# Neighbourhood attention by blocks of grid columns: half the latent keys per query tile

## The chip, the cores and the metric

The kernel runs on one core of one Trainium2 chip. The metric is the device time of one execution in microseconds (us); lower is better. The engines are TensorE (PE, its weight loads PEld), VectorE (DVE), ScalarE (ACT), GpSimd (POOL) and SyncE (SP, which issues most DMAs).

## The reference

Two layers of a hybrid transformer over 512 latent tokens (a grid of 8 rows by 64 columns, numbered row by row) and 256 context tokens, width 1024. Each layer normalises the tokens, projects them once, splits the projection among four attention branches, gates and merges the branches, projects back, and then runs a mixture of 32 experts. The branches have four query heads of 64:

- A: latent attention with a low-rank key and value, dense over all keys;
- B: banded: a latent query sees latent keys at a distance of at most 128, and a sink logit;
- C: two-dimensional neighbourhood: with 8 rows the window takes in every row, and 16 columns;
- D: dense, with normalised and rotated queries and keys.

A latent query reads its latent keys and all 256 context keys in one softmax; context queries read only context keys (in layer 0 alone). For branch C, cut to what matters:

```python
c_start = jnp.clip(q_col - NA_KW // 2, 0, GRID_W - NA_KW)          # NA_KW = 16, GRID_W = 64
col_ok = (k_col[None] >= c_start[:, None]) & (k_col[None] < c_start[:, None] + NA_KW)
bias = rpb[:, dr, dc]                  # learned, by row and column distance
s = q @ [keys, context keys] * scale + [bias, 0];  s = where(mask, s, -1e30);  p = softmax(s);  o = p @ values
```

A query in column c so reads keys of columns within some 8 of c, 16 columns of 64, in all 8 rows.

## The kernel before

Weights and activations are kept as two parts, H (rounded to TensorE's fp32r) and L (the remainder), and a product is the sum of three (`mm3`, L305: H.H, H.L, L.H). The normalised tokens lie transposed in `hlat` (latent tokens, 512 columns in token order) and `hctx` (context tokens); `hsl` (L557) takes a slice of them.

A layer has a dense part (`dense`, L501: norms, projections, attention, gates, merge), an output projection (`out_proj`, L1178) and the experts (`moe`). In the dense part TensorE runs its instructions in the order in which the program writes them (`manual_schedule`, L471); the other engines' orders are the compiler's. A planner (`Flow`, L142) sets that written order: work is cut into items (`Item`, L136) with dependencies, a latency to keep after them, a need for PSUM banks and a number of SBUF slots. It keeps a model clock `clk`, to which each product adds its modelled time (`mat`, L243), and models when banks come free from tuned latencies (`LT`, L1878). When no item can go on, it puts in a piece of the filler: the gate projections with, in layer 0, the modulation products (`gates`, L1061, `mod_seg`, L397). The filler also runs ahead of ready items up to a share (`FILL`, 0.8 in layer 0 and 0.4 in layer 1) of the main work done. So the order of all attention work hangs on the modelled lengths.

Branch C (`branch_c`, L717) runs in two halves of two heads. Per half `qk` (L721) projects queries and keys transposed (`projT`, L575: weights stationary, 512 latent columns of `hlat` moving; result 128 channels by 512 tokens in one bank) and writes them with one ScalarE and one VectorE pass per head and part. The values of both halves come from `val` (L741): per token tile of 128 the tokens are stationary and 256 weight columns move, and two ScalarE copies write `V`. `bias_c` (L994) loads per head a table of 896 columns by a POOL-queue DMA and folds the column mask in on VectorE.

`attend` (L959) makes for each group g of 256 queries (g = 0, 1 latent, g = 2 context) two query tiles of 128 times two heads. Per tile `scores` (L1002):

- multiplies the query tile with the keys, latent and context columns apart, two products each (high and low key part; three in branch A), into one of two buffers `sps`. Branch C sees 512 latent columns, branch B 384 (`kts`, L967), the ends of the band masked;
- takes the minimum (scores are negated): for B and C over the context part (L1023), then a pass that adds the bias or the band mask and takes the minimum over the latent part (L1030);
- takes the exponent with the sum (L1040), the reciprocal (L1044) and the division (L1045) into `P`;
- transposes `P` by 128 columns on TensorE, three to a bank (L1056), and evicts each bank to `PT` on ScalarE (L1057).

`values` (L979) then multiplies `PT` with `V`, one key tile after the other from 0 on, both heads side by side in the array, 256 queries to a product, in plain float; one VectorE copy (L989) takes the sum out of the bank to the buffer `oT` (one of the eight of tag `t1`) and SP stores it in DRAM (L990). The merge (`merge`, L1093) reads these tensors back in the order B, A, C, D (L1111) after the attention. The trace counts two entries for each plain-float product.

## Time and profile before

| | |
|---|---|
| median of 3 runs | 2233.65 us (2231.22 to 2238.22) |
| the profiled execution | 2233.26 us |
| its span, first to last instruction | 2231.2 us |
| mean granted TensorE clock | 0.969 |
| busy: PE / PEld | 2071.0 us (93%) / 1529.6 us (69%) |
| busy: DVE / ACT / POOL | 1292.9 us (58%) / 798.7 us (36%) / 306.4 us (14%) |
| moved by DMA | 431.44 MB |

Busy time is the time in which an engine has at least one instruction under way; the shares are of the span. The clock is given as a share of full speed, 2.4 GHz. All that follows is worked out on the profiled execution.

### The profile page before, as it was taken

What the parts mean: (1) busy time and instruction counts of PE and PEld (TensorE: products, weight loads), DVE (VectorE), ACT (ScalarE), POOL (GpSimd) and SP (SyncE); (2) the same over time, 40 slices, a digit from 0 to 9 for tenths busy, and PEclk for the clock granted to TensorE, in tenths of its full rate; (3) what the DMA queues carried; (4) which work ended last, traced back from release to release, by engine and by line L of the source; (5) the groups of instructions that cost most, each with busy time, mean ns of one, the idle gap of its engine ahead of it and who ended that gap; (6) DMA issues with size and microseconds to landing.
All of it is one profiled execution on the core that took longest, in us unless ns stands there. A gap on an engine that the chain in (4) does not pass through costs nothing. (4 is left out here: it accounts for less than half of the span.)

```text
span 2231.2 us, 34132 instructions
## 1 busy us (share of the span) xinstructions
PE 2071.0 (93%) x13033; PEld 1529.6 (69%) x13033; DVE 1292.9 (58%) x2641; ACT 798.7 (36%) x1805; POOL 306.4 (14%) x325
## 2 busy tenths in 40 slices
PE   5899999999999997969999979999999998799997
PEld 2777877787888877934444468877888787644443
DVE  2545354436555565677777766555466466746655
ACT  2345355435445221212222235465455432212112
POOL 1301100001100144230000031000020013200000
PEclk8899999999999999979999989999999999899999
DMA  8234343433414655679999423112212377699992
GB/s 288 93 135 171 112 163 133 159 133 135 137 60 121 201 192 198 228 255 405 364 365 364 176 78 106 54 48 90 90 46 86 121 259 250 239 369 408 407 408 88
DMA packets 141925, 431.44 MB, mean 193 GB/s; under 512 B 19328, under 2 KB 32016, under 8 KB 141760
## 3 DMA queue, kind: packets, MB, share of 16 engines
q1 hardware_dynamic: 127264, 388.89, 48.1%
q0 software_dynamic: 13056, 35.10, 4.8%
q10 hardware_dynamic: 1440, 5.24, 0.6%
q8 instruction: 104, 1.70, 0.3%
q14 instruction: 61, 0.50, 0.1%
HBM read 399.19 MB, written 36.78 MB: 195 GB/s over the span
## 5 line engine op out<-in xcount | busy, mean ns | idle before, releaser
L250 PE MATMUL bk<-hT,wH 128*128 128x512 f32 (+1 forms) x1760 | 481.5, 361 | 5.8 <-ACT wH L274 4.6
L250 PEld LDWEIGHTS bk<-hT,wH 128*128 128x128 f32 x1760 | 299.7, 190 | 53.3 <-issue 9.0
L250 PE MATMUL bk<-hT,wL 128*128 128x512 f32 (+1 forms) x880 | 312.1, 355 | 2.8 <-DVE wL L275 2.8
L250 PE MATMUL bk<-wH,hT 128*128 128x256 f32 x1312 | 257.0, 290 | 3.8 <-DVE hT L550 1.9
L1674 DVE TENSOR_TENSOR x<-x,sps 128x1024 f32<-128x1024 f32 x166 | 195.4, 1216 | 100.4 <-PE sps L1673 99.8
L1615 PE MATMUL bk<-e,xT 128*64 128x512 f32 x1056 | 244.8, 601 | 0.0
L250 PEld LDWEIGHTS bk<-wH,hT 128*128 128x128 f32 x1312 | 213.2, 195 | 9.3 <-DVE sk L275 2.1
L275 DVE TENSOR_TENSOR wL<-wraw,wH 128x1024 fp32r<-128x1024 f32 x112 | 141.7, 1272 | 108.5 <-PE bk L250 56.1
L250 PE MATMUL bk<-wL,hT 128*128 128x256 f32 x656 | 187.9, 286 | 0.0
L250 PEld LDWEIGHTS bk<-hT,wL 128*128 128x128 f32 x880 | 166.4, 189 | 29.2 <-DVE wL L275 5.6
L274 ACT ACTIVATE wH<-wraw 128x1024 fp32r<-128x1024 f32 x132 | 138.5, 1058 | 133.3 <-DMA wraw<-in_w_gate_dram 40.3
L1615 PEld LDWEIGHTS bk<-e,xT 128*64 128x64 f32 x1056 | 72.0, 138 | 142.0 <-issue 127.5
L1040 ACT ACTIVATE P<-sps,m 128x768 f32<-128x768 f32 (+2 forms) x160 | 126.4, 791 | 75.0 <-DVE m L1020 50.8
L1673 PE MATMUL sps<-yeH,to 128*128 128x512 f32 x332 | 142.0, 428 | 2.8 <-ACT yeH L274 1.4
L1057 ACT ACTIVATE pt<-bk 128x384 f32<-128x384 f32 (+1 forms) x288 | 121.0, 466 | 65.5 <-PE bk L255 64.7
L321 POOL TENSOR_TENSOR rr<-rs,mhalf 128x1 f32<-128x1 f32 (+1 forms) x72 | 53.9, 750 | 611.1 <-DVE rs L317 537.8
L1673 PE MATMUL sps<-yeL,to 128*128 128x512 f32 x332 | 131.2, 395 | 1.7 <-DVE yeL L275 1.7
L255 PE MATMUL bk<-ident,P 128*128 128x128 f32 x800 | 119.1, 277 | 12.3 <-ACT pt L1057 5.5
L250 PEld LDWEIGHTS bk<-wL,hT 128*128 128x128 f32 x656 | 128.2, 195 | 0.5
L1638 PE MATMUL bk<-e,gT 128*64 128x512 f32 x528 | 122.3, 606 | 1.5 <-ACT gT L1631 1.5
L255 PEld LDWEIGHTS bk<-ident,P 128*128 128x128 f32 x800 | 90.8, 140 | 39.5 <-ACT pt L1057 10.8
L1621 ACT ACTIVATE eth<-bk 128x256 f32<-128x256 f32 x33 | 12.7, 384 | 284.5 <-PE bk L1615 284.5
(331 smaller groups left out, 3637.0 us busy)
## 6 DMA issues: line engine op xcount, KB each, us to landing
e<-in_w_dram SPq DMA_DIRECT2D x384, 512.0 KB
wmod<-in_w_mod_dram SPq DMA_DIRECT2D x96, 512.0 KB
wraw<-in_w_gate_dram SPq DMA_DIRECT2D x64, 512.0 KB
wraw<-in_w_in_dram SPq DMA_DIRECT2D x36, 512.0 KB
thd<-th SPq DMA_DIRECT2D x64, 256.0 KB
thm<-thd SPq DMA_DIRECT2D x32, 384.0 KB
wraw<-in_w_br_dram SPq DMA_DIRECT2D x16, 512.0 KB
wraw<-in_w_out_dram SPq DMA_DIRECT2D x16, 512.0 KB
```

Source lines behind the costliest of these rows:

```text
L250: return self.nc.tensor.matmul(out, lhsT, rhs, **kw)
L255: return self.nc.tensor.transpose(out, src, self.ident if ident is None else ident)
L274: nc.scalar.activation(H, src, AF.Copy)
L275: (eng or nc.vector).tensor_tensor(L, src, H.bitcast(F32), op=ALU.subtract)
L321: self.nc.gpsimd.tensor_tensor(r[:, :n], o[:, :n], self.mhalf.to_broadcast([128, n]), op=ALU.pow)
L1040: nc.scalar.activation(Pt[:, :n], S[:, lo:768], AF.Exp, scale=-1.0, bias=m, accum_out=sm)
L1057: nc.scalar.activation(PT[gi][:, :w, qi * 128:(qi + 1) * 128], v, AF.Copy)
L1615: nc.tensor.matmul(box["h"][64 * z:64 * z + 64, :], xT(k, z), W(z, k // 2)[:, (k % 2) * 512:(k % 2 + 1) * 512], start=k == 0, stop=k == 7, ...
L1621: nc.scalar.activation(th[s], H[s, :256], AF.Tanh, scale=0.5)
L1638: nc.tensor.matmul(Y[n][64 * z:64 * z + 64, :], gT[:, k, 64 * z:64 * z + 64], W(z, 4 + k)[:, n * 512:(n + 1) * 512], start=k == 0, stop=k ...
L1673: nc.tensor.matmul(ps[:, c], to[s, t * 128:(t + 1) * 128], w[s, c], start=i == 0, stop=i == 1)
L1674: nc.vector.tensor_tensor(self.x1[t] if out is None else out, self.x1[t], ps, op=ALU.add)
```

## The change

The latent tokens of branch C are taken in the order (block of 8 grid columns, row, column in block) instead of row by row. Queries are kept rotated by one block, so that query tile u holds the blocks 2u+1 and 2u+2 (the last one 7 and 0), and sees two key tiles of 128: u and u+1, the last one 0 and 3. The order arises in the projection, which reads `hlat` by columns (`by_column`); the values are projected transposed like the keys and turned back on TensorE (`valT`). One bias table per head serves the three inner tiles and one the wrapped tile; both heads' tables are one load of 1024 columns with the mask in it, negated on ScalarE. In branch B the first and the last query tile see two key tiles instead of three. `values` starts with key tile 4 and ends with 5, and gives a key tile's product only those queries that see it. The neighbourhood output is put back into row order by four copies and by the store. The constant `cmask` goes. Cut to its core:

```diff
+    blk = lambda cbs: (np.repeat(np.arange(8)[None], 8, 0).T[None].repeat(len(cbs), 0).reshape(-1),
+                       (8 * np.array(cbs)[:, None, None] + np.arange(8)[None, None]).repeat(8, 1).reshape(-1))
+    tabs = []
+    for qb, kb in (((1, 2), (0, 1, 2, 3)), ((7, 0), (0, 1, 6, 7))):
+        (qr, qc), (kr, kc) = blk(qb), blk(kb)
+        c0 = np.clip(qc - 8, 0, 48)[:, None]
+        ok = (kc[None] >= c0) & (kc[None] < c0 + 16)
+        dc = np.clip(kc[None] - qc[:, None], -15, 15) + 15
+        tabs.append(np.where(ok, rpb_c[:, :, kr[None] - qr[:, None] + 7, dc], np.float32(-BIG)))
+    r["rpb"] = f(np.stack(tabs, 3).reshape(NL, 2, 2, 128, 512).transpose(0, 1, 3, 2, 4).reshape(NL, 2, 128, 1024))
...
+    def by_column(self, hl, k, t0, n):
+        if t0 >= 512:
+            return self.hsl(hl, k, t0, n)
+        return self.hlat[hl][k // 2][:, k % 2].rearrange("p (r b c) -> p b r c", r=8, b=8)
...
         ps = self.bank()
         c = slice(c0, c0 + 128)
-        self.mm3(ps[:, :n], [(W(0, k)[:, c], W(1, k)[:, c], self.hsl(0, k, t0, n), self.hsl(1, k, t0, n))
-                             for k in range(8)])
+        out = ps[:, :n]
+        if t0 == 0:
+            out = out.rearrange("p (b r c) -> p b r c", r=8, c=8)
+        self.mm3(out, [(W(0, k)[:, c], W(1, k)[:, c], self.by_column(0, k, t0, n), self.by_column(1, k, t0, n))
+                       for k in range(8)])
         return ps
...
                 if part == 0:
                     q = hf.q(t0, n)
-                    nc.scalar.activation(q[own, j], ps[own, :n], AF.Copy, scale=-0.125)
-                    nc.vector.scalar_tensor_tensor(q[oth, j], ps[own, :n], -0.125, q.bitcast(F32)[own, j],
-                                                   op0=ALU.mult, op1=ALU.subtract)
+                    for d, s, m in ((0, 64, 448), (448, 0, 64)) if t0 == 0 else ((0, 0, n),):
+                        d, s = slice(d, d + m), slice(s, s + m)
+                        nc.scalar.activation(q[own, j, d], ps[own, s], AF.Copy, scale=-0.125)
+                        nc.vector.scalar_tensor_tensor(q[oth, j, d], ps[own, s], -0.125, q.bitcast(F32)[own, j, d],
+                                                       op0=ALU.mult, op1=ALU.subtract)
...
+        def valT(i):
+            ps = self.projT(box["u", 5], 128 * i, 0, 512)
+            f.use("bk", self.LT["cacc"])
+            vT = [self.t1("vT") for _ in range(2)]
+            for z in range(2):
+                nc.scalar.activation(vT[z], ps[:, 256 * z:256 * z + 256], AF.Copy)
+            yield self.LT["kt"], ("bk",)
+            v = self.transposed([vT[t // 2][:, t % 2 * 128:t % 2 * 128 + 128] for t in range(4)])
+            f.use("bk", self.LT["vacc"])
+            nc.scalar.activation(box[i].V[:, 0:4], v, AF.Copy)
         vals = []
         for hb in range(2):
             load, new = self.load_unit(box, 4 + 2 * hb), self.new_half(box, hb, "m")
-            bias = f.item(self.nop(0, lambda hb=hb: box.__setitem__(("bt", hb), [self.bias_c(2 * hb + j)
-                                                                                for j in range(2)])), slots=2)
+            bias = f.item(self.nop(0, lambda hb=hb: box.__setitem__(("bt", hb), self.bias_c(hb))), slots=1)
             pre = [load, new, bias]
             ps = []
             for t0, n in ((0, 512), (512, 256)):
...
                 new1 = self.new_half(box, 1, "m", "v")
                 new1.slots = 0
                 lv = self.load_unit(box, 5)
-                vals = [f.item(val(t), deps=[lv, new, new1], lat=self.LT["load"], need=("bk",)) for t in range(6)]
+                vals = [f.item(v, deps=[lv, new, new1] + self.norms, lat=self.LT["load"], need=("bk",))
+                        for v in [valT(i) for i in range(2)] + [val(t) for t in (4, 5)]]
                 pre += [new1, lv]
                 proj += vals + [f.item(self.nop(4), deps=vals)]
-            out.append((pre, proj, lambda hb=hb, ps=ps: self.attend("c", 2, hb, box, ps + vals, None), 7))
+            out.append((pre, proj, lambda hb=hb, ps=ps: self.attend("c", 2, hb, box, ps + vals, None), 6))
         return out
...
+    def keys(self, br, u):
+        if br == "b":
+            return list(range(max(u - 1, 0), min(u + 2, 4)))
+        if br == "c":
+            return [u, u + 1] if u < 3 else [0, 3]
+        return list(range(4))
     def attend(self, br, n, hb, box, qs, ks):
         f = self.fl
         items = []
         for g in range(3 if self.wc else 2):
-            kts = [4, 5]
-            if g < 2:
-                kts = list(range(g, g + 3) if br == "b" else range(4)) + kts
-            groups = [kts[i:i + 3] for i in range(0, len(kts), 3)]
+            see = [self.keys(br, 2 * g + qi) + [4, 5] if g < 2 else [4, 5] for qi in range(2)]
+            kts = [t for t in see[0] if t < 4] + [t for t in see[1] if t < 4 and t not in see[0]] + [4, 5]
+            groups = [kts[:-2], [4, 5]] if len(kts) == 5 else [kts[i:i + 3] for i in range(0, len(kts), 3)]
             PT = [[], []]
             tiles = []
             for qi in range(2):
-                deps = qs if ks is None else [qs[2 * g + qi]] + [ks[t] for t in kts]
+                deps = qs if ks is None else [qs[2 * g + qi]] + [ks[t] for t in see[qi]]
                 for j in range(2):
-                    tiles.append(f.item(self.scores(br, hb, box, j, g, qi, groups, PT[j]), deps=deps, lat=self.LT["evac"],
-                                        need=("S", "P")))
-            items += tiles + [f.item(self.values(n, hb, box, g, kts, PT), deps=tiles, lat=self.LT["pv"], need=("bk",))]
+                    tiles.append(f.item(self.scores(br, hb, box, j, g, qi, see[qi], groups, PT[j]), deps=deps,
+                                        lat=self.LT["evac"], need=("S", "P")))
+            items += tiles + [f.item(self.values(br, n, hb, box, g, see, groups, PT), deps=tiles, lat=self.LT["pv"],
+                                     need=("bk",))]
         return items
-    def values(self, n, hb, box, g, kts, PT):
-        f, hf = self.fl, box[hb]
+    def values(self, br, n, hb, box, g, see, groups, PT):
+        f, hf, nc = self.fl, box[hb], self.nc
         acc = self.bank()
         f.use("bk", self.LT["oacc"])
-        for i, kt in enumerate(kts):
+        at = [(gi, i, kt) for gi, grp in enumerate(groups) for i, kt in enumerate(grp)]
+        at = at[-2:-1] + at[:-2] + at[-1:]
+        for gi, i, kt in at:
+            q = [qi for qi in range(2) if kt in see[qi]]
+            c = slice(128 * q[0], 128 * q[-1] + 128)
             for j in range(2):
-                self.mat(acc[64 * j:64 * j + 64, :256], hf.v(j, kt), PT[j][i // 3][:, i % 3, :],
-                         start=i == 0, stop=i == len(kts) - 1, tile_position=(0, 64 * j))
+                self.mat(acc[64 * j:64 * j + 64, c], hf.v(j, kt), PT[j][gi][:, i, c],
+                         start=kt == 4, stop=kt == 5, tile_position=(0, 64 * j))
         f.left["pt1"] += len(PT[0]) + len(PT[1])
         oT = self.t1("oT")
-        self.nc.vector.tensor_copy(oT, acc[:, :256])
-        self.nc.sync.dma_start(self.ob[n][hb][:, g * 256:(g + 1) * 256], oT)
+        out = self.ob[n][hb]
+        if br == "c" and g < 2:
+            rows = oT.rearrange("p (r b c) -> p r b c", r=8, b=4)
+            src = acc[:, :256].rearrange("p (b r c) -> p b r c", b=4, r=8)
+            for b in range(4):
+                nc.vector.tensor_copy(rows[:, :, b], src[:, b])
+            grid = out[:, :512].rearrange("p (r c) -> p r c", r=8)
+            for b, m, c0 in ((0, 4, 8),) if g == 0 else ((0, 3, 40), (3, 1, 0)):
+                nc.sync.dma_start(grid[:, :, c0:c0 + 8 * m], oT.rearrange("p (r x) -> p r x", r=8)[:, :, 8 * b:8 * b + 8 * m])
+            return
+        nc.vector.tensor_copy(oT, acc[:, :256])
+        nc.sync.dma_start(out[:, g * 256:(g + 1) * 256], oT)
         return
         yield
-    def bias_c(self, h):
...
-    def scores(self, br, hb, box, j, g, qi, groups, PT):
+    def bias_c(self, hb):
+        bt = self.slot(name="bt")
+        self.nc.gpsimd.dma_start(bt, self.a["rpb"][self.l, hb])
+        self.nc.scalar.activation(bt, bt, AF.Copy, scale=-1.0)
+        return bt.rearrange("p (j w k) -> p j w k", j=2, w=2)
+    def scores(self, br, hb, box, j, g, qi, see, groups, PT):
         nc, f, hf = self.nc, self.fl, box[hb]
         lat = g < 2
-        k0, kn = (g * 128, 384) if br == "b" else (0, 512)
-        lo = 512 - kn if lat else 512
-        q0 = g * 256 + qi * 128
+        u = 2 * g + qi
+        kts = see[:-2]
+        kn = 128 * len(kts)
+        lo = 512 - kn
         S = self.sps()
         f.use("S", self.LT["S"] + (self.LT["Sb"] if br in "bc" and lat else 0.0))
         f.left["P"] -= 1
-        q = hf.q(q0, 128)[:, j]
-        for c0, cn, kk in ([(lo, kn, k0)] if lat else []) + [(512, 256, 512)]:
-            self.mat(S[:, c0:c0 + cn], q, hf.kh(0, j, kk, cn), start=True, stop=False)
-            self.mat(S[:, c0:c0 + cn], q, hf.kh(1, j, kk, cn), start=False, stop=br != "a")
+        wrap = br == "c" and u == 3
+        q = hf.q(u * 128, 128)[:, j]
+        for c0, cn, k0 in ([(lo, kn, 128 * kts[0])] if lat else []) + [(512, 256, 512)]:
+            out = S[:, c0:c0 + cn]
+            if wrap and k0 == 0:
+                out = out.rearrange("p (t n) -> p t n", t=2)
+                kk = lambda z: hf.kh(z, j, 0, 512).rearrange("p (t n) -> p t n", t=4)[:, 0:4:3]
+            else:
+                kk = lambda z: hf.kh(z, j, k0, cn)
+            self.mat(out, q, kk(0), start=True, stop=False)
+            self.mat(out, q, kk(1), start=False, stop=br != "a")
             if br == "a":
-                self.mat(S[:, c0:c0 + cn], hf.qr(q0, 128)[:, j], self.KR[:, kk:kk + cn], start=False, stop=True)
+                self.mat(out, hf.qr(u * 128, 128)[:, j], self.KR[:, k0:k0 + cn], start=False, stop=True)
         m = self.tiny.tile([128, 1], F32, name="m", tag="m", bufs=4)
         if br in "ad" or not lat:
             nc.vector.tensor_reduce(m, S[:, lo:768], axis=AX.X, op=ALU.min)
...
             m0 = self.tiny.tile([128, 1], F32, name="m0", tag="m0", bufs=4)
             nc.vector.tensor_reduce(m0, S[:, 512:768], axis=AX.X, op=ALU.min)
             if br == "b":
-                o = {0: 2, 1: 1, 2: 1, 3: 0}[2 * g + qi]
-                bias = self.bmask[:, o * 128:o * 128 + 384]
+                o = 128 * (kts[0] - u) + 256
+                bias = self.bmask[:, o:o + kn]
             else:
-                u = 7 - 2 * (2 * g + qi) - 1
-                bias = box["bt", hb][j][:, u:u + 8].rearrange("p u c -> p (u c)")
+                bias = box["bt", hb][:, j, int(wrap)]
             nc.vector.tensor_tensor_reduce(out=S[:, lo:512], in0=S[:, lo:512], in1=bias, op0=ALU.add,
                                            op1=ALU.min, scale=1.0, scalar=m0, accum_out=m)
         if br == "b":
...
             elif qi == 0:
                 PT += [self.sm.tile([128, 3, 256], F32, name="pt", tag="pt", bufs=NPT) for _ in groups]
                 f.left["pt1"] -= len(groups)
-            w = len(grp)
+            own = [i for i, kt in enumerate(grp) if kt in see]
+            i0, w = own[0], len(own)
             f.use("bk", self.LT["pt"])
-            v = self.transposed([Pt[:, (gi * 3 + i) * 128:(gi * 3 + i + 1) * 128] for i in range(w)])
-            nc.scalar.activation(PT[gi][:, :w, qi * 128:(qi + 1) * 128], v, AF.Copy)
+            v = self.transposed([Pt[:, see.index(grp[i]) * 128:see.index(grp[i]) * 128 + 128] for i in own])
+            nc.scalar.activation(PT[gi][:, i0:i0 + w, qi * 128:(qi + 1) * 128], v, AF.Copy)
         f.left["P"] += 1
```

## Rows read from the trace of the kernel before

**Rows 1.** Busy time by engine in stretches of the span (windows).

```profile
core 0: us, PE busy (x) PEld busy (x) DVE busy (x) ACT busy (x) POOL busy (x), PEclk, DMA share, GB/s
...
100.00:800.00 700.00, 688.58 (x4893) 568.63 (x4892) 351.89 (x826) 313.60 (x760) 70.40 (x101) 1.00 0.42 144
...
1300.00:1875.00 575.00, 545.57 (x3362) 461.02 (x3362) 336.83 (x745) 278.32 (x645) 62.06 (x64) 0.99 0.31 103
```

**Rows 2.** Instructions on tile `th`: count, duration ns min/median/max, first and last start.

```profile
L1087 ACT ACTIVATE th<-bk,hb x96: 454/687/725, 95.6 to 1852.7; 128x512 f32<-128x512 f32 x64, 128x256 f32<-128x256 f32 x32
```

**Rows 3.** PE's waits, 1325 to 1850 us: total us, times, longest us.

```profile
PE bk L255 <- ACT pt L1057: 4.7, 9, 1.1
```

**Rows 4.** Timeline of PE, layer 0's branch C: start us, us, instructions merged.

```profile
490.96 1.15 PE L255 MATMUL bk<-ident,P 128*128 128x128 f32 x9
491.86 0.71 PE L250 MATMUL bk<-hT,wH 128*128 128x512 f32 x2
...
492.64 0.39 PE L250 MATMUL sps<-kh,sq 128*128 128x512 f32 x1
492.87 0.39 PE L250 MATMUL sps<-kl,sq 128*128 128x512 f32 x1
493.09 0.28 PE L250 MATMUL sps<-sc,sq 128*128 128x256 f32 x1
...
493.33 0.63 PE L250 MATMUL bk<-hT,wH 128*128 128x512 f32 x2
...
494.11 2.81 PE L250 MATMUL bk<-pt,V 128*64 128x256 f32 x24
496.86 0.73 PE L250 MATMUL bk<-hT,wH 128*128 128x512 f32 x2
```

**Rows 5.** Timeline of PE, layer 0's branch B.

```profile
133.20 0.51 PE L250 MATMUL sps<-sk,sq 128*128 128x384 f32 x2
133.55 0.40 PE L250 MATMUL sps<-sc,sq 128*128 128x256 f32 x2
133.79 0.40 PE L250 MATMUL bk<-hT,wH 128*128 128x256 f32 x2
```

**Rows 6.** Timeline of all engines around one call of `values`.

```profile
423.79 3.33 PE L250 MATMUL bk<-pt,V 128*64 128x256 f32 x24
...
425.07 0.49 ACT L1057 ACTIVATE pt<-bk 128x384 f32<-128x384 f32 x1
```

**Rows 7.** Groups by line and form: count, busy us, mean ns, idle before and releasers.

```profile
L255 PE MATMUL bk<-ident,P 128*128 128x128 f32 x800 | 119.1, 277 | 12.3 <-ACT pt L1057 5.5 <-DVE rs L317 2.0 <-ACT V L683 1.6
...
L1057 ACT ACTIVATE pt<-bk 128x384 f32<-128x384 f32 x224 | 100.7, 490 | 55.0 <-PE bk L255 54.6
...
L250 PE MATMUL bk<-pt,V 128*64 128x256 f32 x800 | 96.2, 384 | 0.0
...
L250 PEld LDWEIGHTS bk<-pt,V 128*64 128x64 f32 x800 | 54.2, 136 | 34.3 <-issue 4.0 <-ACT pt L1057 1.6 <-ACT sq L616 0.7
...
L1030 DVE CUSTOM_DVE_ANT_0 sps<-sps,bt,m 128x512 f32<-128x512 f32 x32 | 24.3, 758 | 1.0
...
L1057 ACT ACTIVATE pt<-bk 128x256 f32<-128x256 f32 x64 | 23.5, 382 | 10.4 <-PE bk L255 10.1
...
L1030 DVE CUSTOM_DVE_ANT_0 sps<-sps,bmask,m 128x384 f32<-128x384 f32 x32 | 20.0, 624 | 0.6
...
L989 DVE COPY oT<-bk 128x256 f32<-128x256 f32 x40 | 16.9, 422 | 38.9 <-PE bk L250 38.6
```

**Rows 8.** Groups by line and form, DVE alone (L603 reads runs of 8, L601 of 32).

```profile
L603 DVE TENSOR_TENSOR r<-bk,rope_a 128x32 f32<-128x32 f32 x32 | 4.6, 181 | 0.1
...
L601 DVE TENSOR_TENSOR r<-bk,rope_a 128x32 f32<-128x32 f32 x8 | 1.4, 180 | 0.0
```

**Rows 9.** DMA issues: count, KB each, median us from issue to landing.

```profile
bt<-in_rpb_dram POOLq DMA_DIRECT2D x8, 448.0 KB, 3.5
...
rcol<-modd POOLq DMA_DIRECT2D x6, 4.0 KB, 6.8
```

More of the change, by code (lines that the diff above doesn't have):

```diff
@@ L59, in consts @@
     cs = np.clip(qc - 8, 0, 48)
-    c["cmask"] = np.where((kc >= cs) & (kc < cs + 16), 0.0, BIG).astype(np.float32)
     c["tri"] = (a < b).astype(np.float32)
@@ L113, in prep @@
     r["sink"] = f(sink_b)
-    pad = np.zeros((NL, 4, 15, 128), np.float32)
-    pad[..., 48:79] = rpb_c
-    qc, kc = np.arange(64)[:, None], np.arange(64)[None, :]
-    sk = pad[..., kc - qc + 63]
-    bt = np.stack([sk[:, :, 1:15], sk[:, :, 0:14]], 2)
-    r["rpb"] = f(bt.transpose(0, 1, 2, 4, 3, 5).reshape(NL, 4, 128, 14 * 64))
+    blk = lambda cbs: (np.repeat(np.arange(8)[None], 8, 0).T[None].repeat(len(cbs), 0).reshape(-1),
[8 more added lines that the diff above has]
+    r["rpb"] = f(np.stack(tabs, 3).reshape(NL, 2, 2, 128, 512).transpose(0, 1, 3, 2, 4).reshape(NL, 2, 128, 1024))
     r["g_qd"], r["g_kd"] = f(g_q_d), f(g_k_d)
@@ L359, in rest @@
             self.bmask = ld("bmask", [128, 640])
-            self.cmask = ld("cmask", [128, 64])
             self.iota = ld("iota", [128, 64])
@@ L991, in values @@
+        nc.vector.tensor_copy(oT, acc[:, :256])
+        nc.sync.dma_start(out[:, g * 256:(g + 1) * 256], oT)
         return
         yield
-    def bias_c(self, h):
-        nc = self.nc
-        bt = self.slot(name="bt")[:, :896].rearrange("p (u c) -> p u c", u=14)
-        nc.gpsimd.dma_start(bt.rearrange("p u c -> p (u c)"), self.a["rpb"][self.l, h])
-        nc.vector.scalar_tensor_tensor(bt, bt, -1.0, self.cmask[:, None, :].to_broadcast([128, 14, 64]),
-                                       op0=ALU.mult, op1=ALU.add)
-        return bt
```

## The prediction, made before the changed kernel was run

> **What bounds the kernel now.** I read the stretches first [rows 1]. From 100 to 800 us (layer 0's projections, attention and most of its merge) TensorE is busy 688.58 of 700 us, from 1300 to 1875 us (the same work of layer 1) 545.57 of 575, at a granted clock of 1.00 and 0.99, so at the 2.4 GHz level. VectorE has 351.89 and 336.83 us in these stretches, ScalarE 313.60 and 278.32, the DMA engines a share of 0.42 and 0.31: TensorE alone is full. The reason is in the code: the planner fills every gap of the attention with the gate projections. Next I looked for the point at which this filling runs out. The activations that end the gates' products run from 95.6 to 1852.7 us [rows 2], so there is a gate product to put into a gap until the merge's last branch, in both layers. What TensorE does wait for is spread thin: in layer 1 the largest entry is 4.7 us for the eviction of transposed probabilities, nine times [rows 3]. So a microsecond of TensorE work taken out of attention should come off the time almost whole, unless what is left waits longer. The expert stages in between are not touched; I take their time as it is, since what is saved ahead of them only shifts them.
>
> **The change part by part.** Prices are distances between starts in the timeline, since printed durations of matmuls overlap.
>
> Neighbourhood scores. Per tile the two 512-column products become two of 256. The two wide ones take 492.64 to 493.09, 0.45 us, the two narrow ones behind them 0.24 [rows 4], so 0.21 us less. There are 2 layers x 2 halves x 4 query tiles x 2 heads = 32 such tiles, as the 32 biased reductions confirm [rows 7]: 6.7 us.
>
> Neighbourhood transposes. Six per tile become four. Nine cost 0.90 us [rows 4], 0.10 each: 64 x 0.10 = 6.4 us.
>
> Neighbourhood probabilities times values. One call is 12 products (24 entries) in 494.11 to 496.86, 2.75 us [rows 4], 0.46 per key tile with both heads. Six key tiles of 256 queries become three of 256 and two of 128, worth four: 2 x 0.46 x 8 calls = 7.3 us.
>
> Banded ends. In 16 of the 32 tiles 384 columns become 256. Two 384-column products take 0.35 us, two of 256 0.24 [rows 5]: 16 x 0.11 = 1.8 us. One transpose less in each: 1.6 us. In each of 8 calls one key tile serves half the queries: 8 x 0.23 = 1.8 us.
>
> Values of the neighbourhood branch. Per layer 4 x 24 products of 256 columns (0.12 us, as the narrow scores) become 2 x 24 of 512 (0.225): 11.5 us become 10.8. Eight transposes come in, 0.8 us. Both layers: 0.2 us more.
>
> TensorE's work thus falls by 25.6 - 0.2 = 25.4 us, if each piece keeps its price.
>
> What comes in beside it. (a) Each of the 40 value calls now starts with key tile 4, whose probabilities are transposed last, and no longer with tile 0. In one call today the products start at 423.79, while that eviction begins only at 425.07 and takes 0.49 us [rows 6]; in the new order TensorE would stand from 423.79 to about 425.6, 1.8 us. Today's weight loads of these products lose 1.6 us in all to these evictions [rows 7], so such calls are few. Bounds: 0, and eight such calls, 14 us; I take 2, nearest to the second row, as the planner's distance ahead of a value call stays. (b) A neighbourhood value call frees its PSUM bank after four copies of 64 columns instead of one of 256. One copy of 256 takes 422 ns [rows 7], one VectorE pass of 32 columns 180 [rows 8]; four of 64 are then some 0.85 us by estimate, 0.43 later, 8 x 0.43 = 3.4 us if TensorE always waited for that bank; there are four, so I take 1; the low end is 0. (c) VectorE and ScalarE get lighter: 512 to 384 columns took the biased reduction from 758 to 624 ns, so 256 should take some 490, and an eviction falls from 490 to 382 [rows 7]. A score chain shortens by about a microsecond. The planner's latencies stay as they were, so the products are not asked for earlier, but will find their input ready more often; up to the 4.7 us of [rows 3] could go. I take 0. (d) The query block is written rotated, in two pieces of 448 and 64: eight more pairs of small ScalarE and VectorE passes, of the kind of 0.18 us [rows 8], with both engines half idle [rows 1]; if that cover failed, 8 x 0.4 = 3 us. (e) Bias: four loads on POOL's queue for eight, four ScalarE passes over 1024 columns for eight on VectorE; the tables are asked for halves ahead; ScalarE is strictly in order, but a table takes 3.5 us to land [rows 9] and is started long before. Cost nothing; if it stood ahead of an eviction, 3.5 us each. One slot less per half only gives the planner room. (f) Stores: per half and layer the two stores of 128 KB in rows of 1 KB become three with runs of 128, 96 and 32 bytes, 1024 runs each. On SP's queue this is four issues more in all, and the gate loads behind them are prefetched. The nearest rows: 1024 pieces of 4 bytes land in 6.8 us, 448 KB in long rows in 3.5 [rows 9], so some 3.3 us later or, low end, no later. Nothing reads these tensors until the merge; a late store only keeps one of eight staging buffers. I take 0; the high end, 12 x 3.3 = 40 us, would need TensorE to stand behind each, and I count one or two, 5 us, as its end.
>
> Sum: 25.4 - 2 - 1 = 22.4 us. The profiled execution took 2233.26 us, its span 2231.2 and 2.1 around it, 0.4 under the median of the runs; 2233.26 - 22.4 = **2211 us**. The terms' milder and harsher ends give 2203 to 2222 for this case.
>
> **The rivals.**
>
> Slower: the permuted read. The latent query, key and value projections now stream their 512 columns in runs of 8 floats that lie 64 floats apart. These are 4 x 24 + 2 x 24 = 144 products per layer, 288 in all, at 0.225 us. If each took 78 ns longer, the gain is gone; if the stream halved its rate, 288 x 0.225 = 65 us come on, 2276 us. The far end is the unrounded float rate of the value products, 0.46 us per 256 columns, so 0.92 per 512: 200 us more. No row shows TensorE reading in short runs. VectorE does: a pass over 32 columns in runs of 8 takes 181 ns, one over 32 in a row 180 [rows 8]. That is another engine, so the case keeps a tenth. The Trainium skill, "SBUF — State Buffer", section "Door 1: The DMA port swizzle", says that SBUF is read in lines of 16 bytes and that two reads in a line suffice for full rate. Eight floats fill two lines, so by that rule this rival would not occur; no run here shows it for TensorE.
>
> No change worth the name: waits take the gain. Mechanism: the planner's tuned latencies and orders no longer fit, and TensorE, which keeps its written order, stands where (a), (b) and (f) say. Two thirds of the gain lost gives 2226, all of it 2233; I write 2228. For: TensorE already has 29.4 us without work in layer 1's stretch [rows 1]. Against: each chain gets shorter, none longer, apart from the bank and the stores. The Trainium skill, "DMA: Bandwidth & Descriptors", section "Specifications", says that transfers under 512 bytes become read-modify-writes; by that rule the stores would be the ones that bite, and the time would go to this rival's. No row here times such a store.
>
> More than the work: shorter score chains also take out waits. If half of layer 1's 29.4 us went as well, 2211 - 15 = 2196.
>
> **How the numbers follow.** The forecast has 0.70, the lost gain 0.12, the permuted read 0.10, the larger gain 0.08. The likeliest time is 2211. From 2198 to 2228 lie all of the first case, half of the lost gain and five eighths of the larger one, 0.81 in all. About 0.3% (6.7 us) is what a measurement can tell from no change: faster means below 2227. That is 0.70 + 0.08 + half of 0.12 = 0.84; the other half, 0.06, is no change; 0.10 slower.
>
> **What would show it right or wrong.** In the changed profile: transposes of probabilities fall from 800 entries to 720, value products from 800 to 768 [rows 7], the 256-column products of the value projection by 192, the 512-column ones rise by 96; the wide-score pairs of the neighbourhood take 0.24 us instead of 0.45. TensorE's busy time in layers 0 and 1 ahead of the experts falls by some 25 us, its share stays at 98 and 95%. The forecast is wrong if a 512-column product of the query projection starts its successor more than 0.3 us later, if TensorE's idle time in the two stretches (11.4 and 29.4 us) grows by over 10 us, or if the expert stages change in length.

## The result, and the profile after

The changed kernel takes 2256.34 us (median of 4 runs, 2252.09 to 2264.16) against 2232.43 of the kernel before in the same session: a ratio of 1.0102, 95% interval 1.0086 to 1.0118. It is slower by 1.0%, where 2211 was forecast. The profiled execution took 2257.95 us. One execution of an experiment below (`f2_before_tr`, 2399.31 us at a granted clock of 0.831) fell in a slower state of the chip, and its ratio leaves it out.

First the work. The page's busy row of the changed kernel, then two windows that answer to [rows 1] (columns as there):

```profile
span 2256.0 us, 33769 instructions
...
PE 2066.0 (92%) x12841; PEld 1514.7 (67%) x12841; DVE 1270.0 (56%) x2665; ACT 788.5 (35%) x1813; POOL 307.6 (14%) x321
```

```profile
100.00:800.00 700.00, 668.69 (x4656) 542.27 (x4655) 328.23 (x830) 300.73 (x756) 59.62 (x93) 0.99 0.42 135
1300.00:1875.00 575.00, 535.08 (x3252) 445.76 (x3253) 335.23 (x757) 279.07 (x655) 61.14 (x57) 0.99 0.31 99
```

In both stretches TensorE stands still longer: 31.3 us of the first where it was 11.4, and 39.9 of the second where it was 29.4 (the second window holds some 25 us more of the stage ahead of layer 1 than it did before). No other engine has taken over; DVE and ACT have become lighter. The groups by line and form, answering to [rows 7], and the stores and the bias table, answering to [rows 9], show that the edits did what the diff says:

```profile
L258 PE MATMUL bk<-ident,P 128*128 128x128 f32 x720 | 112.4, 281 | 21.7 <-ACT pt L1111 11.5 <-DVE P L1098 4.1 <-DVE r L614 2.1
...
L253 PE MATMUL bk<-pt,V 128*64 128x256 f32 x672 | 89.4, 391 | 2.5 <-ACT pt L1111 2.5
...
L1111 ACT ACTIVATE pt<-bk 128x384 f32<-128x384 f32 x144 | 64.5, 489 | 38.0 <-PE bk L258 37.4
...
L1111 ACT ACTIVATE pt<-bk 128x256 f32<-128x256 f32 x144 | 49.9, 381 | 42.1 <-PE bk L258 41.7
...
L1083 DVE CUSTOM_DVE_ANT_0 sps<-sps,bt,m 128x256 f32<-128x256 f32 x32 | 15.2, 489 | 0.6
...
L253 PE MATMUL bk<-pt,V 128*64 128x128 f32 x96 | 10.6, 273 | 0.0
...
L1031 DVE COPY oT<-bk 128x64 f32<-128x64 f32 x32 | 5.0, 216 | 3.2 <-PE bk L253 3.1
```

```profile
o<-oT SPq DMA_DIRECT2D x36, 128.0 KB, 1.9
...
bt<-in_rpb_dram POOLq DMA_DIRECT2D x4, 512.0 KB, 3.9
o<-oT SPq DMA_DIRECT2D x4, 96.0 KB, 2.3
o<-oT SPq DMA_DIRECT2D x4, 32.0 KB, 2.6
```

There are 720 transposes instead of 800 and 768 value entries instead of 800 (two to a product), 96 of them over 128 queries. But 12.3 us of waiting ahead of the transposes have become 21.7, with the eviction `pt` first among the releasers.

Where on the time line the loss arises follows from the starts of marked instructions in each trace: a transpose of the normed rows (in layer 0 the first, in layer 1 the last), then the first and the last product on `oHL` with `wH` (the merge). All in us; the last two rows are experiments told below.

| kernel | layer 0 to its merge | merge 0 | layer 1 to its merge | merge 1 |
|---|---|---|---|---|
| before | 679.1 | 111.3 | 454.6 | 93.6 |
| changed | 695.3 | 122.2 | 446.4 | 101.4 |
| changed, before's order | 675.0 | 111.8 | 446.7 | 95.3 |
| before, changed order | 699.8 | 123.9 | 463.0 | 98.8 |

Layer 1's attention is 8.2 us shorter, where half of the forecast's 25.4 was to go. Layer 0's is 16.2 longer, and the merges 10.9 and 7.8. The stages between and behind keep their length within 2.5 us.

Part of this is work that has moved: in the changed kernel more of the gate projections are left for the merge. Their entries with the high weight part in merge 0, before and changed:

```profile
L250 PE MATMUL bk<-hT,wH 128*128 128x512 f32 x64 | 20.0, 394 | 0.0
...
L250 PE MATMUL bk<-hT,wH 128*128 128x256 f32 x65 | 12.0, 283 | 0.0
```

```profile
L253 PE MATMUL bk<-hT,wH 128*128 128x512 f32 x74 | 23.0, 393 | 0.0
...
L253 PE MATMUL bk<-hT,wH 128*128 128x256 f32 x80 | 14.8, 283 | 0.0
```

With the low part these are 16 entries of 512 columns and 22 of 256 more, at 0.227 and 0.12 us by estimate 16 x 0.227 + 22 x 0.12 = 6.3 us, which layer 0's attention has less to do. In layer 1 nine entries of 512 columns, 2.0 us, have moved the same way. At equal gate work layer 0's attention is thus some 22 us longer, not 16, and its merge 5, not 11. So the question is what layer 0 lost. PE's waits in layer 0's attention, before and changed (us in total, times, longest):

```profile
PE bk L255 <- ACT pt L1057: 0.8, 3, 0.4
...
PE bk L250 <- ACT pt L1057: 0.5, 1, 0.5
```

```profile
PE bk L258 <- ACT pt L1111: 6.4, 11, 1.6
PE bk L258 <- DVE P L1098: 4.1, 2, 3.7
PE bk L253 <- ACT pt L1111: 2.9, 4, 1.3
PE bk L253 <- ACT wH L277: 2.1, 1, 2.1
PE sps L253 <- ACT P L1093: 2.0, 1, 2.0
```

And TensorE's clock: before's is granted at 1.00 from 100 to 800 us [rows 1]. In the changed kernel four stretches of layer 0's attention are at 0.50, the 1.2 GHz level; the first and the last of them:

```profile
255.70:259.10 3.40, 3.24 (x15) 3.24 (x16) 1.60 (x9) 1.10 (x5) 0.55 (x1) 0.50 0.02 6
...
692.60:702.80 10.20, 6.45 (x22) 5.21 (x21) 8.47 (x13) 8.21 (x16) 0.00 (x0) 0.50 0.29 93
```

The timeline ahead of the longer one shows how a wait comes about:

```profile
686.97 1.06 ACT L277 ACTIVATE oHL<-orw 128x1024 fp32r<-128x1024 f32 x1 [5.01 <-DMA orw<-o]
...
688.06 1.23 DVE L278 TENSOR_TENSOR oHL<-orw,oHL 128x1024 fp32r<-128x1024 f32 x1 [5.78 <-ACT oHL L277]
...
689.20 1.81 DVE L1074 TENSOR_REDUCE m<-sps 128x1 f32<-128x768 f32 x2
690.18 0.90 ACT L1093 ACTIVATE P<-sps,m 128x768 f32<-128x768 f32 x1 [2.16 <-DVE m L1074]
...
691.23 0.73 PE L253 MATMUL sps<-sk,sq 128*128 128x512 f32 x2 [1.96 <-ACT P L1093]
...
696.91 1.30 PE L258 MATMUL bk<-ident,P 128*128 128x128 f32 x5 [3.75 <-DVE P L1098]
```

A merge load of an earlier branch stands in branch D's attention. ScalarE does nothing for 5.01 us until that transfer has landed; VectorE stands behind it for the low part of the same split; the softmax comes late, and TensorE waits for it twice (1.96 and 3.75 us). Before's order has the same load in branch D's attention too, but there ScalarE waits 0.23 us for it:

```profile
672.10 1.06 ACT L274 ACTIVATE oHL<-orw 128x1024 fp32r<-128x1024 f32 x1 [0.23 <-DMA orw<-o]
```

What stands beside what is the planner's decision. Its lengths for the changed items changed, and from 116 us on the two traces show TensorE's instructions in another order.

### The profile page after: what moved, and what is told of

The parts are those of the page before. It is cut to its first block, busy times and chain, and to the rows that moved or that the text cites. A ratio compares the mean times of both kernels' runs of the same rounds, so it can differ in the third digit from the quotient of the medians.

```text
span 2256.0 us, 33769 instructions
## 1 busy us (share of the span) xinstructions
PE 2066.0 (92%) x12841; PEld 1514.7 (67%) x12841; DVE 1270.0 (56%) x2665; ACT 788.5 (35%) x1813; POOL 307.6 (14%) x321
## 5 line engine op out<-in xcount | busy, mean ns | idle before, releaser
L253 PE MATMUL bk<-hT,wH 128*128 128x512 f32 (+1 forms) x1824 | 507.7, 366 | 6.6 <-ACT wH L277 5.7
L253 PEld LDWEIGHTS bk<-hT,wH 128*128 128x128 f32 x1824 | 315.3, 191 | 62.3 <-issue 10.5
L253 PE MATMUL bk<-hT,wL 128*128 128x512 f32 (+1 forms) x912 | 328.2, 360 | 8.8 <-DVE wL L278 8.8
L253 PE MATMUL bk<-wH,hT 128*128 128x256 f32 x1184 | 234.9, 292 | 3.1 <-DVE hT L552 1.6
L253 PEld LDWEIGHTS bk<-wH,hT 128*128 128x128 f32 x1184 | 194.2, 196 | 7.2 <-DVE hT L552 1.8
L253 PE MATMUL bk<-wL,hT 128*128 128x256 f32 x592 | 170.1, 287 | 0.0
L1093 ACT ACTIVATE P<-sps,m 128x768 f32<-128x768 f32 (+3 forms) x160 | 117.7, 737 | 60.7 <-DVE m L1074 44.2
L258 PE MATMUL bk<-ident,P 128*128 128x128 f32 x720 | 112.4, 281 | 21.7 <-ACT pt L1111 11.5
L1074 DVE TENSOR_REDUCE m<-sps 128x1 f32<-128x768 f32 (+1 forms) x96 | 73.2, 776 | 77.7 <-PE sps L253 77.1
L258 PEld LDWEIGHTS bk<-ident,P 128*128 128x128 f32 x720 | 81.7, 141 | 52.4 <-ACT pt L1111 23.9
L253 PEld LDWEIGHTS bk<-wL,hT 128*128 128x128 f32 x592 | 116.4, 197 | 0.2
```

Source lines behind the costliest of these rows:

```text
L253: return self.nc.tensor.matmul(out, lhsT, rhs, **kw)
L258: return self.nc.tensor.transpose(out, src, self.ident if ident is None else ident)
L1074: nc.vector.tensor_reduce(m, S[:, lo:768], axis=AX.X, op=ALU.min)
L1093: nc.scalar.activation(Pt[:, :n], S[:, lo:768], AF.Exp, scale=-1.0, bias=m, accum_out=sm)
```

## The experiments

The kernel before, run beside them, had a median of 2236.91 us with the runs e, 2231.92 with f, 2237.03 with g and 2233.66 with h.

| run | median, us | ratio to before (95%) |
|---|---|---|
| e1_pin: change, before's order | 2219.68 | 0.9924 (0.9899 to 0.9948) |
| e2_shared: change, early start of `values` | 2260.63 | 1.0108 (1.0082 to 1.0135) |
| e3_pin_shared: both | 2219.39 | 0.9924 (0.9900 to 0.9947) |
| e4_no_band: branch C's part alone | 2251.52 | 1.0066 (1.0037 to 1.0095) |
| f1_short: before's work, changed order | 2278.71 | 1.0200 (1.0172 to 1.0227) |
| f2_before_tr: before, one planner number | 2253.41 | 1.0083 (1.0052 to 1.0114) |
| f3_after_tr: change, the same number | 2260.58 | 1.0115 (1.0086 to 1.0145) |
| f4_plain: e1_pin without permuted reads | 2214.70 | 0.9924 (0.9897 to 0.9952) |
| g1_pin_L0: before's order in layer 0 only | 2225.85 | 0.9961 (0.9946 to 0.9976) |
| g2_orw_pool: change, merge loads on POOL's queue | 2259.41 | 1.0105 (1.0078 to 1.0133) |
| g3_pin_orw: the same on e1_pin | 2223.50 | 0.9941 (0.9918 to 0.9965) |
| h1_after_pt: change, LT pt raised | 2255.04 | 1.0090 (1.0071 to 1.0109) |

**The order against the work.** `e1_pin` makes the whole change but charges the planner before's lengths and slots:

```diff
@@ def scores
+        full = {"b": 3}.get(br, 4) if lat else 0
+        f.clk += 2 * 0.425 * 128 * (full - len(kts))
...
+            if lat and br in "bc":
+                f.clk += 109.0 * ((1 if gi else 3 - w) if br == "c" else len(grp) - w)
@@ def values
+        want = {"b": 10, "c": 12}.get(br, 0) if g < 2 else 0
+        f.clk += want * (0.47 * 256 + 5.0) - (f.clk - clk0 if want else 0.0)
```

The bias item is charged two slots again, and a half gives back seven. The value projection is cut into six items as before's was, with `valT`'s transposes uncharged in the last two. `clk0` is the planner's clock at the start of `values`.

> The whole change, but the planner is charged before's lengths and slots for the changed items (and the V projection is cut into the same six items), so that the items stand in TensorE's instruction stream exactly in before's order. ORDER (my theory): the 24 us lost, and the 14 to 16 us of work really saved that do not show, both come from the new order, which meets late evictions in layer 0 and a held DMA queue in the merge; with before's order the time is 2232 - 15 = 2217 (2208 to 2226), TensorE's clock stays at 1.00 from 100 us to the end of layer 0's attention, and the idle time of TensorE there is back near 13 us (32 in the changed kernel). LATE START (values begin with the key tile whose eviction is last): that part is still in, time 2245 to 2256, waits on pt as in the changed kernel. WORK (permuted reads, short bursts, four copies cost more than they save): nothing of it is taken out, 2253 to 2260.

Measured: 2219.68, a ratio of 0.9924. The order is before's: up to the experts of layer 1, the traces show TensorE's tiles in the same sequence but for the value projections. The page's busy row has the changed kernel's instruction counts on every engine, and its busy times but for TensorE's, which is 10 us lower, in 37 us less of span:

```profile
span 2218.7 us, 33778 instructions
...
PE 2055.7 (93%) x12841; PEld 1514.0 (68%) x12841; DVE 1269.5 (57%) x2665; ACT 788.9 (36%) x1813; POOL 307.3 (14%) x321
```

Its waits in layer 0's attention are near before's:

```profile
PE bk L253 <- ACT pt L1126: 2.0, 3, 1.2
...
PE bk L258 <- DVE P L1111: 0.9, 1, 0.9
PE bk L258 <- ACT th L1156: 0.9, 2, 0.6
...
PE bk L258 <- ACT pt L1126: 0.7, 3, 0.3
```

The same stretch in the windows, changed kernel and this one:

```profile
100.00:744.00 644.00, 614.78 (x4358) 496.31 (x4357) 296.30 (x788) 288.16 (x741) 50.27 (x85) 0.98 0.40 130
```

```profile
100.00:721.00 621.00, 608.40 (x4369) 495.21 (x4369) 296.23 (x785) 289.56 (x740) 50.86 (x85) 1.00 0.40 134
```

The 23 us between them are 16.6 of idle time (29.2 against 12.6) and 6.4 of TensorE busy longer, at a mean clock of 0.98 instead of 1.00, although the gate work moved to the merge, 6.3 us, is missing from the changed kernel's stretch; `e1_pin` has as much of it in merge 0 as before. One detail missed: the clock does not stay up all the time; one stretch, 307.4 to 310.8 us, is at 0.50, behind waits of 0.8 and 0.9 us.

`f1_short` is the counterpart: before's kernel, with the planner charged the shorter lengths.

```diff
@@ def scores
+        if lat:
+            f.clk -= 2 * 0.425 * (256 if br == "c" else 128 if end else 0)
...
+            if lat and (br == "c" or end and gi == 0):
+                f.clk -= 109.0
@@ def values
+        if g < 2 and br in "bc":
+            f.clk -= 2 * (0.47 * 256 + 5.0) + 4 * 0.47 * 128 if br == "c" else 2 * 0.47 * 128
```

> The kernel before with all its work, but the planner is charged the changed kernel's lengths and slots, so that every item stands in TensorE's stream where the changed kernel has it. One bias tile holds both heads' tables in turn, so both heads of a pair take the second one's table; transfers and instructions are as many as before. ORDER: the changed kernel against its twin in before's order showed that this order costs 37 us, so 2236 + 37 = 2273 (2258 to 2285), with drops of TensorE's clock in layer 0's attention and a merge of layer 0 near 122 us (111 before). A rival, that the new order only hurts together with the new work (two transposes to a bank, and evictions that come sooner): 2232 to 2245.

Measured: 2278.71, 1.0200. TensorE's tiles stand in the changed kernel's sequence but for the value projections. The shared bias tile makes VectorE wait 9.2 us in all for second tables, which the kernel before does not have; no wait of TensorE follows within 15 us of these. So four corners stand. In before's order the new work gains 0.8%, in the changed order 1.0% (1.0200 against 1.0102); the changed order costs the old work 2.0% and the new work 1.8%. The sign of the result is the order's. The rival, that the order hurts only together with the new work, has fallen. The price is not the same everywhere: in layer 1's attention the changed order costs the old work 8.4 us (463.0 against 454.6, with three stretches at 0.50) and the new work nothing (446.4 against 446.7).

**Is before's order special, or the changed one?**

```diff
-            self.fl.clk += 109.0
+            self.fl.clk += 114.0
```

> The kernel before, and only the planner's charge for a transposition is 114 instead of 109 (what the trace shows one to take in layer 1): no work changes, only the order. FRAGILE (the order of before fits closely, and any other order loses): 2240 to 2270. PARTICULAR (only the changed kernel's order is bad, through what became shorter in it): within 5 us of before.

> The changed kernel with the same one number, 114 instead of 109. FRAGILE: another draw, 2225 to 2265, most likely more than 4 us away from 2258. PARTICULAR: 2250 to 2262, with the drops of the clock in layer 0's attention at about the same items.

Measured: the kernel before loses 0.83% through a number that changes no instruction but its place, about as much as the change lost; layer 0 to its merge takes 697.9 us in that trace. FRAGILE holds for before. The changed kernel with it stays at 1.0115, not clearly apart from 1.0102: by its time neither theory is favoured. Its stretches at 0.50 in layer 0's attention begin at 366.2, 530.0, 598.3 and 693.9 us, behind other waits than the changed kernel's (255.7, 429.8, 539.0 and 692.6), which PARTICULAR did not have. `h1_after_pt` tried to mend the planner's picture instead (LT pt 268 and 383, both to 489):

> The changed kernel; the planner's own latency after a probability transposition (LT pt: when the bank is free again) is 489 ns in both layers, what a 384-column eviction takes in the trace, instead of 268 and 383. TUNABLE (the lost time is the planner's wrong picture of these evictions): the 9.3 us of waits on pt in layer 0's attention fall under 4 us and the time is 2235 to 2248. DRAW (no single number brings the fit of before's order back): 2248 to 2265.

Measured: 2255.04; the waits on `pt` are 4.6 and 4.5 us, 9.1 in all against 9.3 in the changed kernel. That is DRAW's range, but hardly a new draw: TensorE's tiles agree with the changed kernel's sequence in 99 of 100 places. What a planner tuned anew would reach is not shown.

**Where the order costs.** `g1_pin_L0` has `e1_pin`'s charges only where `self.wc` is set, in layer 0.

> The whole change, with before's order in layer 0 alone; layer 1's items stand in the changed kernel's order. PLACE (by the stage times of the traces the order costs layer 0 about 20 us in the attention and 10 in the merge, and layer 1 about 6 in its merge): 2219.5 + 6 = 2225 (2220 to 2231). If the loss is spread over both layers, or layer 1 inherits it from layer 0's late end: 2234 to 2245.

Measured: 2225.85. PLACE: some 30 of the 37 us are layer 0's, 6 are layer 1's. In this trace merge 1 is 3.8 us longer than `e1_pin`'s, 2.0 of them the moved gate work.

**The late start of `values`.** `e2_shared` starts with the latent key tile that both query tiles see:

```diff
-        at = at[-2:-1] + at[:-2] + at[-1:]
+        s0 = [kt in see[0] and kt in see[1] for gi, i, kt in at].index(True)
+        at = [at[s0]] + at[:s0] + at[s0 + 1:]
+        first = at[0][2]
-                         start=kt == 4, stop=kt == 5, tile_position=(0, 64 * j))
+                         start=kt == first, stop=kt == 5, tile_position=(0, 64 * j))
```

> The changed kernel, but values begins with the latent key tile that both query tiles see (in the first pt group) instead of key tile 4; all else, the planner's order too, is as changed. LATE START: the waits of TensorE on pt fall from 6.4 us (transposes) and 2.9 us (values) in layer 0's attention to about before's 0.8 and 0.5, the drops of the clock behind them go, and the time is 2220 to 2238. ORDER: the order is the changed one, most waits stay or move to the next user: 2246 to 2260. WORK: 2250 to 2258.

> Both: before's order and the early start of values. ORDER: within 4 us of the run with before's order alone (2208 to 2226). LATE START: at least 10 us under that run. WORK: 2250 to 2258.

Measured: 2260.63 and 2219.39, nothing gained in either order; the first lies 0.6 above ORDER's range. TensorE's tiles stand in the changed kernel's and in `e1_pin`'s sequence. The waits on `pt` in layer 0's attention of `e2_shared` have not gone down from 6.4 and 2.9:

```profile
PE bk L258 <- ACT pt L1113: 6.8, 11, 2.1
PE bk L253 <- ACT pt L1113: 4.4, 3, 3.6
```

LATE START has fallen.

**Branch C alone.** `e4_no_band` lets `keys` return three tiles for branch B, `range(u // 2, u // 2 + 3)`.

> The changed kernel with the banded branch's end tiles back at 384 keys: branch C's part alone. If the parts add up (WORK), the end tiles' saving of about 3 to 5 us is lost: 2259 to 2262. ORDER: the first items of the order are before's again up to branch C, so the drops of the clock at 255.7 and 429.8 us, which stand before any item of C, should be gone or elsewhere, and the time is not tied to the work: 2228 to 2250. LATE START: the start with tile 4 stays, 2250 to 2262.

Measured: 2251.52. With more work in it it is no slower than the changed kernel (the intervals of the two ratios overlap), which speaks against parts that add up. The stretches at 0.50 at 255.7 and 429.8 us are gone, as ORDER had it, and others stand at 315.2, 595.1 and 690.6. But the time is 1.5 us above the range of ORDER and inside that of LATE START, so by itself it settles nothing.

**The loads in the merge.** The longest single wait in the changed kernel's merge 0 (744 to 868 us) is

```profile
PE sps L253 <- ACT wH L277: 8.7, 2, 8.4
```

where `e1_pin` (721 to 835) has

```profile
PE sps L253 <- DVE wL L278: 3.7, 2, 3.1
```

`g2_orw_pool` and `g3_pin_orw` issue `orw` and `orc` with `nc.gpsimd.dma_start`.

> The changed kernel in its own order, but the merge's loads of attention outputs (orw, orc) are issued on POOL's queue instead of SP's. QUEUE (SP holds these loads behind gate loads that wait for a buffer): the 8.4 us gap of TensorE in layer 0's merge and ScalarE's wait of 5.0 us at 682 us go, the merge of layer 0 falls from 122 to about 114 us, the time is 2244 to 2252. CHAIN (the loads wait for their slot or for POOL's own additions just as long): 2253 to 2262, the gap stays.

> The change in before's order, with the same loads on POOL's queue. In that order TensorE waits for no such load, so by both theories nothing changes: 2215 to 2223; a load that POOL issues later than SP did would show as a gap in a merge and 2224 to 2235.

Measured: 2259.41, TensorE's tiles in the changed kernel's sequence. The gap is 6.2 us, and ScalarE's wait for the first of these loads, 5.01 us on SP's queue, is 6.34:

```profile
PE sps L253 <- ACT wH L277: 6.4, 2, 6.2
```

```profile
686.84 1.06 ACT L277 ACTIVATE oHL<-orw 128x1024 fp32r<-128x1024 f32 x1 [6.34 <-DMA orw<-o]
```

CHAIN: another queue doesn't bring these loads forward; the last one is issued at 837.4 us, on SP's queue it was 833.5. On before's order it does not help either (2223.50, just over the range, interval overlapping `e1_pin`'s).

**The price of the permuted reads.** `f4_plain` is `e1_pin` with `by_column` returning `self.hsl(hl, k, t0, n)`, written plainly.

> The change in before's order, but the projections of branch C read the tokens in grid order and write them so (the grouping by blocks is left out, so branch C sees other keys): the price of the permuted reads. By the trace the 144 products per layer took 248 and 256 ns permuted and 238 ns plain, 4 us in all: 2215 to 2217 against 2219.7. If they cost nothing on the path: 2219 to 2221. If they also hold up the evictions: below 2213.

Measured: 2214.70, but the ratio is `e1_pin`'s, 0.9924, so the times don't resolve it. The starts of the same products do. PE's timeline in `e1_pin`, then in `f4_plain`:

```profile
451.88 0.66 PE L253 MATMUL bk<-hT,wH 128*128 128x512 f32 x2
452.38 0.43 PE L253 MATMUL bk<-hT,wL 128*128 128x512 f32 x1
452.64 0.69 PE L253 MATMUL bk<-hT,wH 128*128 128x512 f32 x2
453.16 0.44 PE L253 MATMUL bk<-hT,wL 128*128 128x512 f32 x1
453.44 0.66 PE L253 MATMUL bk<-hT,wH 128*128 128x512 f32 x2
```

```profile
455.24 0.62 PE L253 MATMUL bk<-hT,wH 128*128 128x512 f32 x2
455.69 0.39 PE L253 MATMUL bk<-hT,wL 128*128 128x512 f32 x1
455.92 0.62 PE L253 MATMUL bk<-hT,wH 128*128 128x512 f32 x2
456.37 0.39 PE L253 MATMUL bk<-hT,wL 128*128 128x512 f32 x1
456.60 0.62 PE L253 MATMUL bk<-hT,wH 128*128 128x512 f32 x2
```

Six products take 1.56 us permuted (451.88 to 453.44) and 1.36 plain. Over all ten stretches of permuted products in `e1_pin` the mean distance lies between 240 and 263 ns, 252 on average, against 227 plain: 288 x 0.024 = 7 us. The two attentions of `f4_plain` are 3.5 and 4.0 us shorter than `e1_pin`'s (671.5 and 442.7), which agrees. My expectation of 4 us had compared means that also hold the slower steps of other products.

## Why the prediction was wrong

**The bound** was right: TensorE's work is what counts, and where the order is kept (`e1_pin`) the saving comes off the time: 0.0076 x 2236.91 = 17 us (12 to 23) from 15.5 us of work. The two traces have 12.0 of it in the attentions, 4.1 in layer 0 and 7.9 in layer 1; in layer 0, 1.9 us more of idle time and, by estimate, half of the 3.4 us at 0.50 go against it.

**The terms** against the sums of start distances in the attentions of before and `e1_pin`, both layers: neighbourhood scores 6.7 forecast, 6.7 measured; banded scores 1.8 and 1.8; all transposes of probabilities 8.0 and 7.6; all value products 9.1 and 7.4 (an entry of 128 queries takes 55 to 65 ns, about half of a full one's 116 to 123, and the full ones have become 2 to 4 ns slower); projections 0.2 forecast as a cost, 8.0 measured. The permuted reads make up 7 of these 8, the eight transposes of V per layer 1.5 over both layers. Hence 23.5 - 8.0 = 15.5 instead of 25.4: mis-sized by 10 us, 7 of them in the one rival that I priced but left out of the sum. Its break-even was +78 ns, it measured +24.

**The step that failed** is (c), with the rival "waits take the gain": "the planner's latencies stay as they were, so the products are not asked for earlier, but will find their input ready more often". The latencies do stay, but the lengths that the planner adds up do not, and every later decision hangs on that sum. The changed kernel does not run the old order with shorter pieces; it runs another order, and that costs 37 us (2256.34 against 2219.68), more than the saving. I had "orders no longer fit" as a rival at 0.12, but took TensorE to stand where (a), (b) and (f) say, which the runs do not show (it stands for `pt`, `P` and, in the merge, for weights behind the `orw` loads), and let it take no more than the gain, "all of it 2233". That bound had no reason: an order can lose more than the work saves, as `f2_before_tr` shows with no work saved at all. The argument against it, "each chain gets shorter, none longer", is also only half true: a bank now holds two transposes where it held three, some 0.2 us of TensorE for an eviction of 381 ns. That does not explain the loss, though: `e1_pin` has the same banks and waits 2.7 us for `pt` in layer 0's attention, where the changed kernel waits 9.3. The prediction's own sign did come: idle time up by over 10 us in both stretches (19.9 and 10.5).

**The range** did not follow from its terms either. The harsher ends of (a), (b), (d) and (f) alone add 12 + 2.4 + 3 + 5 = 22 us to 2211, which is 2233 and not 2222.

**The smaller steps.** (a) the late start: no effect (`e2_shared`). (b) the four copies take 216 ns each but overlap, 5.0 us busy in eight calls, so 0.62 us per call and not the 0.85 of the estimate; in `e1_pin` TensorE waits for `oT` in layer 0's attention as often as before, once, for 1.2 us against 1.1. (e) the table lands in 3.9 us, hidden. (f) the stores of 96 and 32 KB land in 2.3 and 2.6 us against 1.9 for the 36 of 128 KB, 32 of them in whole rows; hidden. The Trainium skill, "DMA: Bandwidth & Descriptors", section "Specifications", says that transfers under 512 bytes become read-modify-writes; here such stores landed less than 1 us later. The Trainium skill, "SBUF — State Buffer", section "Door 1: The DMA port swizzle", says that two reads in a line of 16 bytes give full bandwidth. By that rule runs of 8 floats would be read at full rate; 252 against 227 ns does not agree.

**What stays open.** That the granted clock falls because of the waits ahead of it was seen in the traces (each of the four stretches begins within 2 us of the end of a wait of 1.5 to 2.1 us) and not tried by itself; two other waits of 1.5 us in the same attention, which end at 272.7 and 599.1 us, were not followed by a fall. Nor was it tried which of before's many placements makes its order good.

## What to carry to other kernels

Where a planner writes the order from modelled lengths, an edit of a modelled item can deal the order anew, and before's was tuned: the three other orders here (`f2_before_tr`, the changed kernel's, `f3_after_tr`) cost 0.8 to 2.0%, as much as the edit can win or more. Time the edit with the old lengths charged first (same order, less work): that shows what the edit is worth, and here it is also the version to keep: 2219.68 us, 0.8% under the kernel before. Only then tune the planner to the new lengths, and price "the order no longer fits" without letting the gain be its limit.

## What was not expected of the hardware

TensorE reading 512 columns in runs of 8 floats, 64 floats apart, takes 252 ns where a plain read takes 227, 11% more. Four waits of 1.5 to 2.1 us were followed by 3.4 to 10.2 us at the 1.2 GHz level, two others of 1.5 us were not, and in `e1_pin` waits of 0.8 and 0.9 us, one behind the other, were. In layer 0's attention of the changed kernel TensorE was busy 16.33 us of such time, so by estimate half of that, 8 us, is the clock's part of the loss. Four VectorE copies of 64 columns, 216 ns each, start some 0.13 us apart and take 0.62 us together.
